# Twelve row tiles in place of nine, in room taken from the descriptor area of GpSimd's transfers

## The chip, the cores and the metric

The kernel runs on one core of a Trainium2 chip. A core has TensorE (PE in the profile, with its weight loads as PEld), VectorE (DVE), ScalarE (ACT), GpSimd (POOL) and SyncE (SP), which here does nothing but issue transfers between the chip's main memory (HBM) and the on-chip memory (SBUF). Matmuls write to a small memory of eight banks, PSUM. The metric is the device time of one execution in microseconds (us); the times shown are medians of several executions, and the profile is of one of them.

## The reference

One layer of an encoder over 2048 tokens of width 1024 (float32), with 256 memory tokens for the cross-attention. Every sub-layer is wrapped in two RMS norms:

```python
u = rms_norm(h, g_mix_pre);  z = u @ w_in                        # 1024 x 2816
y = concatenate([swa_with_sinks(qa, ka, va, sinks),              # windowed attention
                 hgrn2(qh, fh, ih, gh, lb, onorm)]) @ w_out      # gated recurrence
h = h + rms_norm(y, g_mix_post)
u = rms_norm(h, g_x_pre);    m = rms_norm(mem, g_mem)
h = h + rms_norm(cross_attention(u, m, wq, wk, wv, wo), g_x_post)
u = rms_norm(h, g_ffn_pre)
h = h + rms_norm((silu(u @ w_gate) * (u @ w_up)) @ w_down, g_ffn_post)   # 1024 x 2816 x 1024
```

## The kernel before

All large products are float32 with nearly full precision. Each operand is split into a high and a low part (`split2`, L982: ScalarE or GpSimd rounds the high part, VectorE subtracts it from the whole for the low part), and three matmuls per pair of 128-wide pieces give high x high, high x low and low x high (`products`, L1122 to L1124). Large products are also cut in two by two blocks and done with seven block products in place of eight, with sums and differences of blocks (`seven`, L1126; `streamed` and `combined` make the sums).

The layer is done in three stages. `in_first` (L451) and the stage behind it make the input projection, the windowed attention and the recurrence, and "the fold" (`fold_cross`, L272) multiplies the cross-attention's weights with the memory tokens into two 1024 x 1024 matrices, `qk` and `vo`, in HBM. Beyond the fold, from L253 on, the third stage runs `phases` (L1210) over a list of jobs (`jobs`, L1418): the output projection (`mixed_block`), the scores against `qk` (`score_block`), the values against `vo` (`value_block`), the two halves of the FFN's gate and up products (`hidden_blocks`) and three parts of its down product (`down_block`). Each job holds one operand in SBUF, the other streams by:

- **T tiles** are the resident operand, split. There are seven (four tagged "big", three tagged "T"). To make one, two halves are loaded into row tiles, split by ScalarE (`T<-row`, L985) and VectorE (`T<-row,T`, L988), and given up.
- **sraw** and **S tiles** are the streaming operand, raw and split. A block's `sraw` pair is loaded a block ahead, four such tiles exist, and the S tiles are split two steps ahead.
- **Row tiles** are buffers of 128 x 1024 float32, 4 KB in each partition. `row_tile` (L1458) hands them out in turn from one pool. They are the landing place of T halves and of rows of `x`, `h1` and `h2`, and the place where results are gathered, normed (`squared` L1494, `mean_square` L1472, L1529, L1604, L1617), transposed by TensorE (L1381) with a copy back by ScalarE (L1382), and stored. In the FFN's down part they also are summed into HBM by GpSimd's transfers (`add` L1503, `add_to` L1507), the only transfers that GpSimd issues. A load into a row tile must wait until the tile's last user, often a store, is done.
- **extra** is a single tile of the same size (L84), in which `combined` (L1025) makes the sums of the resident operands beside the earlier jobs and stores them (`qk_s`, `vo_s`, `u_s`, `d_s`; L1032).

`phases` takes each step's transfers, splits and follow-up work in an order written out in code, but the order on each engine is made by a scheduler, which takes the program, the dependencies and its own estimates of time, and places each instruction. SyncE issues its loads (`load`, L74) and stores (`store`, L77) strictly in the order that the scheduler gives, and an issue that must wait holds all that stand behind it.

SBUF is filled to the brim in the third stage. At its lowest addresses lies an area for the descriptors that GpSimd's transfers write, 16 KB of each partition unless the program says otherwise. `cm` (L403 to L408) is a small tile for a causal mask, made by VectorE and GpSimd between the first and the second stage.

Of the kernel before, what the change touches and what calls it, by code (L numbers as in the profile page):

```python
# [11 lines left out]
F32 = mybir.dt.float32  # L12
# [6 lines left out]
P = 128  # L19
T = 2048  # L20
D = 1024
# [27 lines left out]
class Layer:  # L49
# [1407 lines left out]

    def row_tile(self):  # L1458
        self._n += 1
        return self.st_pool.tile([P, D], F32, tag="row", name=f"row_{self._n}", bufs=9)  # L1460

    def rows_of(self, src, n):
        t = self.row_tile()
# [301 lines left out]
```

## Time and profile before

| | |
|---|---|
| median of three executions | 2584.7 us (2578.32 to 2585.96) |
| the profiled execution | 2583.14 us, of which the span from first to last instruction 2581.4 us |
| mean granted TensorE clock | 0.997 of full speed |
| TensorE busy | 2540.2 us, 98% of the span |
| VectorE, ScalarE, GpSimd busy | 1765.3, 1262.4 and 422.6 us |
| moved by transfers | 486.36 MB, 188 GB/s on average |

How to read it: in a row of grouped instructions, `out<-in` names what is written and read, by the program's names without buffer numbers; behind the count come the busy time and the mean of one in ns, then the idle time of the engine just before, and what ended it. In lists of waits, the columns are who waited, for whom, the total in us, how often, and the longest. In lists by time, the columns are start, duration, engine, line, operation; in brackets stands the idle time before and what ended it. In tables by stretch, busy time and count of each engine are followed by the granted clock, the share of the transfer engines' time and the rate.

### The profile page before, as it was taken

The page shows a single profiled execution, that of the slowest core. Times are in us where ns is not written, and L with a number is a line of the kernel's source. Part 1 is how long each engine was busy: PE and PEld are TensorE (multiplying, and loading weights), DVE is VectorE, ACT ScalarE, POOL GpSimd, SP SyncE. Part 2 cuts the span into 40 slices and gives each one's busy share as a digit, 9 for nine tenths or more (in the row PEclk, how much of TensorE's full clock was granted, in tenths as well). Part 3 has the DMA queues.
Part 4 walks back from the last instruction along what each step waited for, and adds up shares of the span by engine and source line. Part 5 has one row for each costly group of instructions (what it writes and reads, how often), then busy time and mean ns, then how long its engine had stood idle before and what let it go on. Part 6 is the DMA issues. An engine that isn't in the chain of part 4 may idle for free.

```text
span 2581.4 us, 34890 instructions
## 1 busy us (share of the span) xinstructions
PE 2540.2 (98%) x12326; PEld 2127.1 (82%) x12326; DVE 1765.3 (68%) x2791; ACT 1262.4 (49%) x2643; POOL 422.6 (16%) x612
## 2 busy tenths in 40 slices
PE   9999999999999999999999999999999999999998
PEld 8888888888988778888778888888888888888886
DVE  7785588987556778778885655566666557574766
ACT  5563466565555565565563333354333335453543
POOL 5231334321302232212300000000000000000022
PEclk9999999999999999999999999999999999999999
DMA  6445755765887886666973622253565425464886
GB/s 188 147 163 178 198 164 158 239 186 175 251 279 283 295 274 217 211 228 200 325 246 127 208 87 74 89 189 130 172 203 196 156 93 190 158 199 106 224 178 152
DMA packets 357295, 486.36 MB, mean 188 GB/s; under 512 B 20352, under 2 KB 248704, under 8 KB 357120
## 3 DMA queue, kind: packets, MB, share of 16 engines
q1 hardware_dynamic: 351072, 462.11, 54.7%
q0 software_dynamic: 6048, 22.02, 4.9%
q8 instruction: 97, 1.59, 0.3%
q14 instruction: 78, 0.64, 0.1%
HBM read 317.34 MB, written 166.72 MB: 188 GB/s over the span
## 4 chain that ended last, share of the span: by engine, by line
PE 83%; DMA 6%; DVE 5%; ACT 3%; issue 2%; SPq 0%; POOL 0%; DVEq 0%; POOLq 0%; ACTq 0%
PE psm L1122 23%; PE psm L1124 23%; PE psm L1123 23%; PE psg L158 2%; PE psg L157 2%; PE psg L156 2%; PE pss L1381 1%; ACT T L985 1%; DMA h1t_d<-row 1%; DMA raw<-in_wo_x_dram 1%; DVE S L988 1%; DMA x<-in_w_out_dram 1%; DMA z<-in_w_out_dram 1%; DMA kk<-z_d 0%; ACT junk L1476 0%
## 5 line engine op out<-in xcount | busy, mean ns | idle before, releaser
L1122 PE MATMUL psm<-T,S 128*128 128x512 f32 x2680 | 1038.3, 392 | 11.4 <-ACT part L1137 9.9
L1123 PE MATMUL psm<-T,S 128*128 128x512 f32 x2680 | 1043.9, 390 | 0.9 <-DVE T L988 0.8
L1124 PE MATMUL psm<-T,S 128*128 128x512 f32 x2680 | 1031.0, 390 | 4.4 <-DVE S L988 4.4
L1122 PEld LDWEIGHTS psm<-T,S 128*128 128x128 f32 x2680 | 504.0, 188 | 120.5 <-ACT part L1137 10.2
L1124 PEld LDWEIGHTS psm<-T,S 128*128 128x128 f32 x2680 | 503.7, 188 | 111.0 <-DVE S L988 6.1
L1123 PEld LDWEIGHTS psm<-T,S 128*128 128x128 f32 x2680 | 504.3, 188 | 105.4 <-DVE T L988 2.3
L985 ACT ACTIVATE S<-sum 128x512 fp32r<-128x512 f32 (+1 forms) x330 | 198.4, 618 | 364.4 <-PE psm L1124 269.5
L988 DVE TENSOR_TENSOR S<-sraw,S 128x512 fp32r<-128x512 f32 (+1 forms) x315 | 214.1, 687 | 227.9 <-ACT S L985 214.2
L988 DVE TENSOR_TENSOR S<-sum,S 128x512 fp32r<-128x512 f32 (+1 forms) x388 | 260.5, 680 | 44.9 <-ACT S L985 29.4
L1137 ACT ACTIVATE part<-psm 128x512 f32<-128x512 f32 x285 | 168.7, 596 | 242.4 <-PE psm L1124 222.6
L985 ACT ACTIVATE S<-sraw 128x512 fp32r<-128x512 f32 (+1 forms) x268 | 165.3, 618 | 105.1 <-PE psm L1124 95.1
L1509 POOL DMA_DIRECT2D y_d<-row x16 | 14.0, 876 | 1076.5 <-DVE row L1695 1025.3
L988 DVE TENSOR_TENSOR T<-row,T 128x1024 fp32r<-128x1024 f32 (+1 forms) x112 | 132.5, 1195 | 40.7 <-ACT T L985 40.4
L157 PE MATMUL psg<-u,whi 128*128 128x512 f32 x320 | 127.8, 399 | 0.0
L158 PE MATMUL psg<-u,wlo 128*128 128x512 f32 x320 | 127.1, 397 | 0.0
L156 PE MATMUL psg<-u,whi 128*128 128x512 f32 x320 | 127.1, 397 | 0.0
L1476 ACT ACTIVATE junk<-row 128x512 f32<-128x512 f32 x160 | 99.7, 624 | 52.3 <-DVE row L1498 31.8
L985 ACT ACTIVATE T<-row 128x1024 fp32r<-128x1024 f32 (+1 forms) x112 | 114.0, 1032 | 17.4 <-DMA row<-d_s 6.6
L987 POOL TENSOR_SCALAR S<-sum 128x512 fp32r<-128x512 f32 x58 | 51.7, 891 | 299.1 <-PE psm L1124 247.1
L1646 DVE TENSOR_TENSOR row<-psm,part 128x512 f32<-128x512 f32 x66 | 43.7, 688 | 68.4 <-PE psm L1124 68.4
L1655 DVE TENSOR_TENSOR part<-psm,part 128x512 f32<-128x512 f32 x66 | 43.8, 688 | 62.7 <-PE psm L1124 62.5
L1695 DVE TENSOR_TENSOR row<-psm,part 128x512 f32<-128x512 f32 x72 | 49.1, 688 | 51.1 <-PE psm L1124 51.0
(364 smaller groups left out, 3710.4 us busy)
## 6 DMA issues: line engine op xcount, KB each, us to landing
sraw<-in_w_gate_dram SPq DMA_DIRECT2D x44, 512.0 KB, 3.6
sraw<-in_w_up_dram SPq DMA_DIRECT2D x44, 512.0 KB, 3.6
hid_d<-row SPq DMA_DIRECT2D x44, 512.0 KB, 2.7
sraw<-hid_d SPq DMA_DIRECT2D x32, 512.0 KB, 4.1
sraw<-in_w_in_dram SPq DMA_DIRECT2D x44, 256.0 KB, 3.4
z_d<-pair SPq DMA_DIRECT2D x20, 512.0 KB, 2.9
raw<-in_w_in_dram SPq DMA_DIRECT2D x20, 512.0 KB, 4.9
z_d<-z SPq DMA_DIRECT2D x20, 512.0 KB, 3.7
```

Source lines behind the costliest of these rows:

```text
L156: nc.tensor.matmul(ps, ah, bh, start=(i == 0), stop=False)
L157: nc.tensor.matmul(ps, ah, bl, start=False, stop=False)
L158: nc.tensor.matmul(ps, al, bh, start=False, stop=(i == n - 1))
L985: self.nc.scalar.activation(hi, raw, AF.Copy)
L987: self.nc.gpsimd.tensor_scalar(hi, raw, 1.0, 1.0, ALU.mult, ALU.mult)
L988: self.nc.vector.tensor_tensor(lo, raw, f32(hi), ALU.subtract)
L1122: nc.tensor.matmul(ps, s[:, 0, k, :], t[:, 0, k, :], start=st, stop=False, **kw)
L1123: nc.tensor.matmul(ps, s[:, 0, k, :], t[:, 1, k, :], start=False, stop=False, **kw)
L1124: nc.tensor.matmul(ps, s[:, 1, k, :], t[:, 0, k, :], start=False, stop=sp, **kw)
L1137: nc.scalar.activation(t, ps, AF.Copy)
L1476: self.nc.scalar.activation(junk, a, AF.Square, scale=float(D) ** -0.5, accum_out=to)
L1695: nc.vector.tensor_tensor(d, a, b, ALU.add)
```

## The change

The pool of row tiles gets twelve buffers in place of nine, 12 KB more in each partition. The room comes from the descriptor area, which is set to 4096 bytes in place of the 16384 that it has without the argument. No other line is changed, but the scheduler makes the order anew from these sizes.

```diff
 def row_tile(self):
     self._n += 1
-    return self.st_pool.tile([P, D], F32, tag="row", name=f"row_{self._n}", bufs=9)
+    return self.st_pool.tile([P, D], F32, tag="row", name=f"row_{self._n}", bufs=12)
...
-    nc = _bacc.Bacc("TRN2", target_bir_lowering=False, num_devices=1)
+    nc = _bacc.Bacc("TRN2", target_bir_lowering=False, num_devices=1, dynamic_dma_scratch_size=4096)
```

In the new order the first 3,800 of TensorE's 11,250 rows (like instructions in a row are one) are the same. VectorE and GpSimd make `cm` a little earlier. In the third stage loads of row tiles move ahead of stores and of stream loads by one to five places on SyncE, above all around the starts of the score, the value and the first FFN job, and splits, transposes and copies follow them.

## The prediction

> **What bounds the kernel now.** I read the page first: its span and its first section.
>
> ```profile
> span 2581.4 us, 34890 instructions
> PE 2540.2 (98%) x12326; PEld 2127.1 (82%) x12326; DVE 1765.3 (68%) x2791; ACT 1262.4 (49%) x2643; POOL 422.6 (16%) x612
> ```
>
> TensorE is busy for 98% of the span, and nothing in the change adds or removes a matmul. All that the change can do is to fill, or to add to, the 41.2 us without one (2581.4 - 2540.2). So I asked next for the busy time by stretch, cut where the losses lie. The load queue's instructions in order of time show the first load of a row tile, at 782.6 us, and so the first cut.
>
> ```profile
> 782.58 0.80 SPq L75 DMA_DIRECT2D row<-out_s  x2
> ```
>
> ```profile
> core 0: us, PE busy (x) PEld busy (x) DVE busy (x) ACT busy (x) POOL busy (x), PEclk, DMA share, GB/s
> 0.00:782.00 782.00, 764.16 (x4348) 660.64 (x4349) 559.85 (x1065) 434.47 (x1035) 228.51 (x340) 1.00 0.63 195
> 782.00:890.00 108.00, 107.91 (x506) 89.34 (x505) 76.40 (x93) 59.08 (x131) 27.48 (x43) 1.00 0.82 285
> 890.00:900.00 10.00, 7.58 (x35) 6.01 (x34) 9.77 (x11) 3.98 (x9) 3.86 (x5) 1.00 0.93 325
> 900.00:950.00 50.00, 50.00 (x238) 41.63 (x237) 34.14 (x39) 29.94 (x68) 13.00 (x21) 1.00 0.86 272
> 950.00:980.00 30.00, 25.59 (x111) 20.13 (x110) 22.17 (x26) 17.54 (x32) 8.05 (x12) 0.89 0.84 305
> 980.00:1130.00 150.00, 149.86 (x720) 124.69 (x719) 115.36 (x209) 86.52 (x210) 40.01 (x55) 1.00 0.64 210
> 1130.00:1260.00 130.00, 128.98 (x608) 106.39 (x607) 109.19 (x143) 75.96 (x172) 35.38 (x48) 1.00 0.70 231
> 1260.00:1340.00 80.00, 75.32 (x346) 61.26 (x345) 69.99 (x79) 55.00 (x106) 17.90 (x25) 0.98 0.88 296
> 1340.00:1735.00 395.00, 395.00 (x1752) 327.23 (x1751) 231.15 (x347) 150.27 (x259) 0.00 (x0) 1.00 0.39 129
> 1735.00:1750.00 15.00, 14.21 (x62) 11.12 (x61) 14.24 (x19) 8.98 (x13) 0.00 (x0) 1.00 0.60 191
> 1750.00:2270.00 520.00, 520.00 (x2295) 430.52 (x2294) 328.89 (x500) 205.91 (x364) 0.00 (x0) 1.00 0.49 166
> ```
>
> From 782 to 2270 us TensorE lacks 0.09 + 2.42 + 0 + 4.41 + 0.14 + 1.02 + 4.68 + 0 + 0.79 + 0 = 13.6 us. In two stretches the granted clock is low as well: 11% of 30 us is 3.3 us, 2% of 80 us is 1.6 us. Together 18.5 us, 0.7% of the span: the ceiling of what more row tiles could bring before 2270 us. Stretches 950-980 (4.41 + 3.3 = 7.7 us) and 1260-1340 (4.68 + 1.6 = 6.3 us) hold most of it. Up to 782 us there are no row tiles at all.
>
> **What it removes: waits for a row tile.** In 950-980 I read the waits of ScalarE (from 900 on), those of the load queue, and then the instructions in order of time.
>
> ```profile
> ACT T L985 <- DMA row<-qk_s: 4.0, 2, 3.3
> ACT T L985 <- DMA row<-qk_d: 3.2, 2, 1.9
> ```
> ```profile
> SPq L75 <- DMA h1t_d<-row: 6.5, 1, 6.5
> SPq L75 <- DVE T L988: 4.7, 4, 2.0
> ```
> ```profile
> 955.47 0.33 SPq L78 DMA_DIRECT2D h1t_d<-row  x1
> 962.40 0.32 SPq L75 DMA_DIRECT2D row<-qk_s  x1
> 962.82 0.39 SPq L75 DMA_DIRECT2D sraw<-h1t_d  x1
> ...
> 966.89 1.06 ACT L985 ACTIVATE T<-row 128x1024 fp32r<-128x1024 f32 x1 [3.29 <-DMA row<-qk_s]
> ...
> 968.58 0.77 PE L1122 MATMUL psm<-T,S 128*128 128x512 f32 x1 [2.68 <-ACT part L1137]
> ```
>
> This is one chain. At 955.5 SyncE issues the store of a row tile. The next load wants that very tile, so the queue stands 6.5 us until the store has landed, and issues the load at 962.4. Its data land at 966.9, where ScalarE, which takes its work in order, has waited 3.3 us to split them. The copy out of PSUM (L1137) stands behind that split, and TensorE waits 2.68 us for the bank. With twelve tiles that load reuses a tile given up three allocations earlier. The changed kernel's order on SyncE says the same: five loads of qk_s and qk_d that stood behind this store or close to it now stand ahead of it, and the stream loads (sraw) behind them.
>
> Can the transfers carry them earlier? By tens of microseconds:
>
> ```profile
> 930.00:940.00 10.00, 10.00 (x50) 8.29 (x49) 5.08 (x6) 8.48 (x19) 3.08 (x7) 1.00 0.75 259
> 940.00:950.00 10.00, 10.00 (x46) 8.29 (x45) 9.26 (x10) 6.03 (x15) 2.69 (x1) 1.00 0.80 254
> 950.00:960.00 10.00, 8.44 (x46) 6.94 (x44) 6.70 (x9) 8.65 (x19) 5.46 (x9) 1.00 1.00 368
> 960.00:970.00 10.00, 7.18 (x27) 5.55 (x28) 9.75 (x9) 5.62 (x9) 2.28 (x1) 0.89 0.66 203
> ```
>
> The engines are full only from 950 to 960. Unused are 2.5 + 2.0 + 0 + 3.4 = 7.9 us, more than the 7.2 us (4.0 + 3.2) that ScalarE waited for these loads. So I take this stretch as won whole: **-7.7 us** (bounds 0, if no load lands sooner, and -7.7).
>
> The low clock belongs to it: gaps of 2.42 us at 893 us left it at 1.00, while here it fell to 0.89 for the stretch. The Trainium skill, "TensorE: Matmul & The Clock Gate", Part 1, says that the clock halves after an idle window of about 3.4 us. By that rule no single gap here is long enough, and the stretch would be worth 4.4 us; the trace shows the clock falling after a gap of 2.68 us, and the measurement decides.
>
> In 1260-1340 only a part is row tiles. The load queue's waits from 1296 to 1316, and the instructions in order:
>
> ```profile
> SPq L75 <- DVE T L988: 8.1, 4, 3.2
> ```
> ```profile
> 1260.07 0.69 DVE L1409 TENSOR_TENSOR row<-row 128x512 f32<-128x512 f32 x1 [2.15 <-DMA u_d<-row]
> ...
> 1311.86 0.50 PE L1122 MATMUL psm<-T,S 128*128 128x512 f32 x1 [2.05 <-ACT part L1137]
> ...
> 1332.28 0.50 PE L1123 MATMUL psm<-T,S 128*128 128x512 f32 x1 [0.76 <-DVE T L988]
> ```
>
> The first wait is for a store of the same tile that is then overwritten (L1409): no number of tiles helps. The second follows loads that waited 8.1 us for VectorE to finish with a tile; their splits then come in a bunch. It and the third cost 2.05 + 0.76 + 1.6 (clock) = 4.4 us. But ScalarE and VectorE are near full here, 55 and 70 of 80 us, so earlier loads spread the bunch only in part. Bounds 0 and -4.4; I take a third, **-1.5 us**, nearer to nothing since the engines are the tighter limit. At 893 us VectorE waits for the one `extra` tile:
>
> ```profile
> 889.67 1.66 DVE L1032 TENSOR_TENSOR extra<-extra,row 128x1024 f32<-128x1024 f32 x1 [2.56 <-DMA qk_s<-extra]
> ```
>
> That tile is not changed: 0. The rest (0.09 + 0.14 + 1.02 + 0.79 = 2.0 us) is small: 0.
>
> **What it adds and moves.** The scheduler was run again, so besides the loads, splits, transposes and sums of score and value blocks change places. On SyncE a stream load now stands behind row loads and stores that wait. The trace of before has no row for the stalls of a new order. Below, a stall is excluded by nothing, and its upper price is the dearest such chain here, 7.7 us; I take **+1.0 us**, the size of the small gaps that lie about (1.02 in 1130-1260).
>
> The mask tile `cm` is made earlier on VectorE and GpSimd, ahead of two weight splits. It ended this wait:
>
> ```profile
> 270.21 0.11 DVE L406 MEMSET cm<- 64x64 f32 x1 [9.37 <-POOL cm L405]
> ```
>
> VectorE had nothing to do then that TensorE lacked; the memset itself is 0.11 us. I take 0; ends: 1 us either way. All left-hand tiles move 12 KB down; no row shows a price of an address: 0.
>
> The smaller descriptor area concerns GpSimd's 42 transfers alone:
>
> ```profile
> q0 software_dynamic: 6048, 22.02, 4.9%
> y_d<-row POOLq DMA_DIRECT2D x16, 512.0 KB, 5.1
> out_dram<-row POOLq DMA_DIRECT2D x14, 512.0 KB, 6.5
> row<-y_d POOLq DMA_DIRECT2D x12, 512.0 KB, 8.2
> ```
> ```profile
> L1509 POOL DMA_DIRECT2D y_d<-row x16: 853/862/1107, 2289.6 to 2424.3; - x16
> ```
>
> They are 6048 / 42 = 144 packets each, 9 for each of 16 engines. The first is issued at 2289.6 us; the room of the 16 sums into y_d, which a smaller area would use again, is free by the landing time of 5.1 us after 2424.3, and the 26 others follow one by one. I take 0; above, one landing time, 8.2 us, if a late transfer had to wait for another and that one ended the kernel. The Trainium skill, "DMA: Bandwidth & Descriptors", Terms, gives a descriptor 16 bytes; by an estimate from that page 4096 bytes would be 256 descriptors, 28 transfers of 9. No run here shows what reuse costs.
>
> **The sum.** -7.7 - 1.5 + 1.0 = -8.2 us on the profiled execution's 2583.1 us (2581.4 of span and 1.7 around it): **2575 us**. That execution lies 1.6 us below the median of the three runs, 2584.7.
>
> **The rivals.**
> - Transfers, not tiles, set the end of 950-980. For it: 368 GB/s and a share of 1.00 at 950-960, right ahead of the gap; loads pulled forward then only queue in the engines. Against it: 0.66 to 0.80 around. Then nothing is won there, and -1.5 + 1.0 gives 2582.6, call it 2583. The Trainium skill, "DMA: Bandwidth & Descriptors", Specifications, puts a core's share of HBM at about 358 GB/s; the 368 here agrees that this window is at the limit.
> - Nearly all of it: the new order also takes the other losses of 1260-1340 (4.4) and the small ones (2.0), with no new stall: 2583.1 - 7.7 - 4.4 - 2.0 = 2569.
> - Slower: a stream load stands behind a row load that waits for its tile. It would happen where score blocks begin. In before the stream load was issued at 962.82 and its pair was first used at 979.80:
>
> ```profile
> 979.80 0.68 DVE L1097 TENSOR_TENSOR sum<-sraw,sraw 128x512 f32<-128x512 f32 x1
> ```
>   With a landing of 5 to 8 us that is some 9 us of slack; the new order puts two more stores and four loads ahead, one of which need only wait the 6.5 us above. From 9 us of delay on, TensorE stops. With the old gap closed, a new one like it, and another at the value blocks, cost 2 x 7.7 against the 7.7 won: 2583.1 + 7.7 = 2591.
>
> **How the numbers follow.** Forecast around 2575 (2571 to 2580): 0.45. Nearly all: 0.15. Transfers set the end: 0.20. Slower: 0.20. A measurement of this kernel can tell about 0.3% from no change, 7.8 us, so faster means below 2577 and slower above 2592.5. Faster: two thirds of the forecast and all of the second, 0.45. Slower: two thirds of the last, 0.14. The rest, 0.41, is within. The range takes in the middle cases and most of both ends: 2565 to 2590.
>
> **What would show it.** In the changed profile: TensorE busy for 29.5 us or more of the 30 around 950-980 and a clock of 1.00 there (the main step); SyncE's wait for h1t_d<-row gone from that stretch; ScalarE's waits for row<-qk_s and row<-qk_d below 2 us together; the wait at L1409 and that at L1032 still there; GpSimd's transfers at 0.9 us of issue and 5 to 8 us to landing as before. Wrong would be the step if the loads are issued earlier and land no earlier (transfers), and the sum if TensorE waits for a stream load.

## The result, and the profile after

| | before | after |
|---|---|---|
| median of 14 executions each | 2580.97 us | 2573.69 us |
| lowest to highest | 2577.73 to 2586.45 | 2568.62 to 2580.88 |
| the profiled execution | 2583.14 us | 2572.97 us |

The ratio of after to before is 0.9963, with a 95% interval of 0.9953 to 0.9973: the change saves 0.37% (0.27 to 0.47), about 9.5 us of the median of before. The medians are 7.3 us apart, the two profiled executions 10.2 us.

The page of after, its span and first section:

```profile
span 2571.3 us, 34876 instructions
...
PE 2535.4 (99%) x12326; PEld 2124.0 (83%) x12326; DVE 1764.8 (69%) x2791; ACT 1263.9 (49%) x2643; POOL 425.4 (17%) x612
```

TensorE now lacks 2571.3 - 2535.4 = 35.9 us, where it lacked 41.2. The busy time by stretch, cut at the same places as before, with the program's first 782 us ahead of the others:

```profile
0.00:782.00 782.00, 764.00 (x4349) 661.00 (x4350) 557.68 (x1065) 435.32 (x1035) 231.45 (x340) 1.00 0.63 195
```
```profile
782.00:890.00 108.00, 105.61 (x492) 87.12 (x491) 76.60 (x92) 59.02 (x130) 29.09 (x42) 1.00 0.81 285
890.00:900.00 10.00, 9.61 (x47) 7.74 (x46) 8.77 (x11) 4.39 (x9) 4.22 (x6) 1.00 0.92 338
...
950.00:980.00 30.00, 30.00 (x149) 24.86 (x149) 27.69 (x34) 24.19 (x53) 11.07 (x17) 1.00 0.83 291
...
1130.00:1260.00 130.00, 127.61 (x597) 105.11 (x598) 110.94 (x138) 73.55 (x166) 38.20 (x52) 1.00 0.70 226
1260.00:1340.00 80.00, 78.48 (x369) 63.87 (x368) 69.01 (x81) 56.33 (x108) 12.50 (x18) 1.00 0.82 278
...
sum 1488.00, PE 1479.69 PEld 1222.47 DVE 1022.95 ACT 703.47 POOL 145.49; mean PE 147.97 PEld 122.25 DVE 102.30 ACT 70.35 POOL 14.55
```

The last row sums the ten stretches from 782 to 2270 us: TensorE lacks 1488.00 - 1479.69 = 8.3 us there, and the granted clock is 1.00 in every one. Before it was 13.6 us idle and 4.9 us of low clock, 18.5. The difference, 10.2 us, is that of the two profiled executions. By stretch, idle and clock together:

| stretch, us | before | after | change |
|---|---|---|---|
| 782-890 | 0.1 | 2.4 | +2.3 |
| 890-900 | 2.4 | 0.4 | -2.0 |
| 950-980 | 7.7 | 0.0 | -7.7 |
| 1130-1340 | 1.0 + 6.3 | 2.4 + 1.5 | -3.4 |
| the other five | 0.9 | 1.6 | +0.7 |

In 950-980 the loads come earlier. The load queue's instructions of after in order of time; before, the load of `qk_s` that ended the wait was issued at 962.40:

```profile
947.21 2.43 SPq L75 DMA_DIRECT2D row<-qk_s  x2
950.75 1.09 SPq L75 DMA_DIRECT2D row<-qk_d  x2
...
954.85 0.33 SPq L78 DMA_DIRECT2D h1t_d<-row  x1
957.66 0.33 SPq L75 DMA_DIRECT2D row<-qk_s  x1
```

The sixth load of `qk_s`, which was issued behind that store at 962.40 and landed at 966.87 before, is now the second of the pair at 947.21: by the trace it is issued at 948.38 and has landed at 957.71. Two loads of `qk_d` (950.75) have passed the store as well, and the next load behind it is issued 2.8 us after it, not 6.9. What is left in 950-980 of the queue's wait for that store (total, how often, longest):

```profile
SPq L75 <- DMA h1t_d<-row: 2.1, 1, 2.1
```

ScalarE's waits for `row<-qk_s` (4.0 us) and `row<-qk_d` (3.2 us) are not in the list of after any more. The room on the transfer engines was used just where it was free:

```profile
930.00:940.00 10.00, 10.00 (x49) 8.28 (x49) 3.97 (x4) 7.89 (x18) 3.08 (x7) 1.00 1.03 387
```

From 930 to 940 us the share rose from 0.75 to 1.03 and the rate from 259 to 387 GB/s. New is a stall at 829.8 us. After's instructions there, the bracket naming the idle time before each:

```profile
821.13 0.36 SPq L75 DMA_DIRECT2D extra<-qk_d  x1
...
826.87 1.23 DVE L1032 TENSOR_TENSOR extra<-extra,row 128x1024 f32<-128x1024 f32 x1 [1.72 <-issue]
...
829.77 0.50 PE L1124 MATMUL psm<-T,S 128*128 128x512 f32 x1 [2.30 <-DVE S L988]
```

In the new order VectorE's sum of `qk` (L1032) stands ahead of the sums and splits of the stream, and its operand, loaded into the one `extra` tile, is issued at 821.1. That is as soon as the store that still held the tile (`qk_s<-extra`, issued at 817.49) has landed, at 821.07 by the trace; the operand lands at 826.79. VectorE waits 1.72 us with all that stands behind it, and TensorE waits 2.30 us for a split. Before, this sum waited too (2.22 us, at 829.01), but behind those splits, and TensorE lost nothing. The two waits that were to stay are there, in another place of the same order:

```profile
889.44 1.23 DVE L1032 TENSOR_TENSOR extra<-extra,row 128x1024 f32<-128x1024 f32 x1 [2.91 <-DMA qk_s<-extra]
...
893.66 0.50 PE L1124 MATMUL psm<-T,S 128*128 128x512 f32 x1 [0.39 <-DVE S L988]
...
1252.21 0.69 DVE L1409 TENSOR_TENSOR row<-row 128x512 f32<-128x512 f32 x1 [1.26 <-DMA u_d<-row]
...
1256.50 0.50 PE L1124 MATMUL psm<-T,S 128*128 128x512 f32 x1 [1.50 <-DVE S L988]
```

### The profile page after: what moved, and what is told of

Read it like the earlier page. It is cut to its first block, busy times and chain, and to the rows that moved or that the text cites. A ratio compares the mean times of both kernels' runs of the same rounds, so it can differ in the third digit from the quotient of the medians.

```text
span 2571.3 us, 34876 instructions
## 1 busy us (share of the span) xinstructions
PE 2535.4 (99%) x12326; PEld 2124.0 (83%) x12326; DVE 1764.8 (69%) x2791; ACT 1263.9 (49%) x2643; POOL 425.4 (17%) x612
## 4 chain that ended last, share of the span: by engine, by line
PE 82%; DMA 6%; DVE 6%; ACT 2%; issue 2%; POOL 1%; SPq 1%; DVEq 0%; POOLq 0%; ACTq 0%
PE psm L1122 22%; PE psm L1124 22%; PE psm L1123 22%; PE psg L157 2%; PE psg L156 2%; PE psg L158 2%; PE pss L1381 1%; DMA x<-in_w_out_dram 1%; DVE S L988 1%; DMA y_d<-sg 1%; DMA u_d<-row 1%; DVE T L988 0%; SPq L75 0%; DMA qk_s<-extra 0%; DVE S L808 0%
## 5 line engine op out<-in xcount | busy, mean ns | idle before, releaser
L1137 ACT ACTIVATE part<-psm 128x512 f32<-128x512 f32 x285 | 168.9, 596 | 244.9 <-PE psm L1124 223.6
L988 DVE TENSOR_TENSOR T<-row,T 128x1024 fp32r<-128x1024 f32 (+1 forms) x112 | 131.8, 1189 | 35.9 <-ACT T L985 34.1
```

What stands on the lines that cost most here:

```text
L988: self.nc.vector.tensor_tensor(lo, raw, f32(hi), ALU.subtract)
L1137: nc.scalar.activation(t, ps, AF.Copy)
```

## The experiments

My theory: loads of T halves wait for a row tile, and each further tile lets them run further ahead; the time comes out of 950 to 1340 us. Rivals: the smaller area itself moves the time; it is not the number of tiles but that loads share tiles with stores; the new order does it by chance, and another one would do as well. Every kernel below was timed against before in five rounds, each pair on one chip; the median of before differs between groups of runs (2581.55 to 2583.49 us), so it is the ratios that can be compared.

### The area alone, and ten and eleven tiles

area_only has nine row tiles as before, and this line alone is changed:

```diff
-    nc = _bacc.Bacc("TRN2", target_bir_lowering=False, num_devices=1)
+    nc = _bacc.Bacc("TRN2", target_bir_lowering=False, num_devices=1, dynamic_dma_scratch_size=4096)
```

rows10 sets `bufs=10` in `row_tile` and the area to 12288, rows11 `bufs=11` and 8192.

> Nine row tiles as before, the descriptor area at 4096 bytes; TensorE's order is that of before, only the mask tile is made earlier. Tiles theory (the time comes from loads that no longer wait for a row tile): no change, ratio 0.999 to 1.001, and the stretch 950-980 us still lacks about 4.4 us of TensorE with a low clock. Area theory (the smaller area, the moved addresses or the earlier mask tile give the time): ratio near 0.996.

> Ten row tiles, area 12288 bytes. Tiles theory: a third of the way or less, ratio 0.998 to 1.000, since one tile more moves the late load of 962.4 us by only one place; the gap near 960 us shrinks but stays. Order theory (each new order by the scheduler gains or loses by chance, the number of tiles does not matter): anything from 0.995 to 1.004, not in step with the number of tiles.

> Eleven row tiles, area 8192 bytes. Tiles theory: between ten and twelve, ratio 0.9965 to 0.999, TensorE's gap near 960 us below 2 us and its clock at 1.00. Order theory: anything from 0.995 to 1.004, not in step with the number of tiles.

| kernel | tiles, area | median, us | ratio to before |
|---|---|---|---|
| area_only | 9, 4096 | 2584.97 (before 2583.19) | 0.9998 (0.9988 to 1.0007) |
| rows10 | 10, 12288 | 2579.2 | 0.9986 (0.9976 to 0.9996) |
| rows11 | 11, 8192 | 2577.68 | 0.9975 (0.9965 to 0.9985) |
| after | 12, 4096 | 2573.69 | 0.9963 (0.9953 to 0.9973) |

From nine to twelve tiles each brings about 0.12%, 3 us, though the intervals of neighbours overlap. The stretch 950-980 of area_only, rows10 and rows11:

```profile
950.00:980.00 30.00, 25.05 (x114) 19.99 (x113) 23.61 (x27) 18.75 (x36) 6.67 (x11) 0.94 0.89 314
```
```profile
950.00:980.00 30.00, 26.17 (x120) 21.46 (x119) 24.08 (x27) 19.81 (x41) 8.34 (x14) 0.94 0.86 310
```
```profile
950.00:980.00 30.00, 27.83 (x133) 22.73 (x132) 25.75 (x32) 22.70 (x48) 13.12 (x17) 1.00 0.74 264
```

TensorE's busy time rises from 25.05 to 26.17, 27.83 and, in after, 30.00 us. ScalarE's waits from 945 to 985 us of area_only and of rows10:

```profile
ACT T L985 <- DMA row<-qk_d: 3.4, 2, 1.8
...
ACT T L985 <- DMA row<-qk_s: 3.2, 1, 3.2
```
```profile
ACT T L985 <- DMA row<-qk_d: 4.2, 2, 2.9
```

With nine tiles both waits of before are there, with ten one of them, with eleven (whose list has none) neither. TensorE's only wait of that stretch in rows11 is for a split by GpSimd, which has nothing to do with row tiles (the last section):

```profile
PE psm L1122 <- POOL S L987: 2.2, 1, 2.2
```

So in this stretch the waits for loads are gone with eleven tiles already, and rows11 missed the gap of under 2 us that was expected of it by another cause. What the twelfth tile adds is not shown: the intervals of rows11 and after overlap.

The area alone does nothing that can be measured, with TensorE's and ScalarE's orders those of before. So the time comes with the tiles and not with the area. Each number of tiles has an order of its own from the scheduler, and no run had twelve tiles in the order of before; what speaks against chance is the series, which goes in step with the number, and the waits that leave with it.

### A smaller area, and a thirteenth tile

rows12_small is after with an area of 1024 bytes, and has its order on every engine; rows13 has thirteen row tiles, for which the area must shrink to 640:

```diff
-        return self.st_pool.tile([P, D], F32, tag="row", name=f"row_{self._n}", bufs=9)
+        return self.st_pool.tile([P, D], F32, tag="row", name=f"row_{self._n}", bufs=13)
...
-    nc = _bacc.Bacc("TRN2", target_bir_lowering=False, num_devices=1)
+    nc = _bacc.Bacc("TRN2", target_bir_lowering=False, num_devices=1, dynamic_dma_scratch_size=640)
```

> Twelve row tiles as in the changed kernel, in the same order, but an area of 1024 bytes, so that its room must be used again many times by the 42 transfers. Tiles theory with a free area: the same as the changed kernel, ratio 0.9953 to 0.9973, GpSimd's transfers at 0.9 us of issue and 5 to 8 us to landing. Area has a price: GpSimd's issue of a transfer grows beyond 1 us or landings beyond 8 us, and if the last ones end the kernel, up to 8 us more (ratio up to 0.9995).

> Thirteen row tiles, area 640 bytes. Tiles theory: the waits for a row tile that cost TensorE time are gone with twelve already, so nothing more: ratio 0.9955 to 0.9975. If more tiles go on helping: the rest of 1260-1340 us (1.5 us) and small gaps go, ratio 0.994 to 0.9955. Order theory: anything from 0.993 to 1.002.

rows12_small: 2573.14 us, 0.9958 (0.9945 to 0.9971), no different from after. rows13: 2581.7 us, 1.0003 (0.9993 to 1.0012): all is lost again. Its 950-980 is still near full (29.84 us busy), and the loss is at the other end of the program:

```profile
2400.00:2555.00 155.00, 150.05 (x655) 123.39 (x654) 102.09 (x138) 72.87 (x144) 30.70 (x44) 0.99 0.77 185
```

In before and after TensorE is busy for all 155 us of that last stretch; here it lacks 5 us. That is where GpSimd's transfers are, so the area of 640 bytes came under suspicion, and was tried by itself below.

### Four tiles for the loads alone

In loads4 the T halves land in four tiles of their own (at all three places that load them), and all else in eight; the area is 4096.

```diff
-        return self.st_pool.tile([P, D], F32, tag="row", name=f"row_{self._n}", bufs=9)
+        return self.st_pool.tile([P, D], F32, tag="row", name=f"row_{self._n}", bufs=8)
+    def half_tile(self):
+        self._n += 1
+        return self.st_pool.tile([P, D], F32, tag="half", name=f"half_{self._n}", bufs=4)
...
-                            half(g, self.row_tile)
+                            half(g, self.half_tile)
```

> The same twelve tiles in two groups: four only for the halves of T tiles, eight for all else. Theory (it is loads queued behind stores of results in one round of tiles that cost the time): the T loads never wait for a store now, the gap near 960 us stays closed, and the ratio is like that of the changed kernel, 0.995 to 0.998. Rival (what counts is how many loads can be ahead): four tiles hold the loads back to four ahead, the waits of ScalarE for row loads come back, and the ratio is 0.999 to 1.006.

2590.84 us, 1.0035 (1.0020 to 1.0049): slower than before with the same twelve tiles. Parting loads from stores did close most of the gap at 950-980 (28.44 us busy, clock 1.00, no wait for `h1t_d<-row`), but time was lost elsewhere, so the idea that it is enough missed. TensorE lacks 2.7 us in 782-890 (at a clock of 0.98) and 4.6 in 2400-2555 (0.99), where before lacks 0.1 and 0 at 1.00. ScalarE's waits of loads4 from 2400 to 2450 us, where before waits 2.4 us for its halves of `d_s`, never over 0.8 at once:

```profile
ACT T L985 <- DMA half<-d_s: 5.9, 4, 3.1
ACT T L985 <- DMA half<-in_w_down_dram: 5.8, 3, 2.2
```

Right behind the longest of them TensorE waits 3.47 us (at 2432.40) for a copy (L1137) that stands behind ScalarE's splits. Four tiles hold two pairs of halves, and no more can be ahead. In one pool of twelve a burst of loads may take more than four when stores are few, and stores when loads are few. So how many loads can be ahead counts as well; but all else had eight tiles here, one fewer than the nine of before, and no run tells the two losses apart.

### A second extra tile

rows9_extra2 has nine row tiles and rows11_extra2 eleven, both with an area of 4096; rows12_extra2 has twelve and an area of 640. All three have

```diff
-        return self.st_pool.tile([P, D], F32, tag="extra", name=f"extra_{self._n}", bufs=1)
+        return self.st_pool.tile([P, D], F32, tag="extra", name=f"extra_{self._n}", bufs=2)
```

> Nine row tiles as before, two extra tiles, area 4096 bytes. Theory: the wait at 893 us (2.4 us) goes, the gap at 950-980 us (7.7 us) stays, since that is the row tiles': ratio 0.998 to 1.000. Rival (any 4 KB more for any tile gives the gain, by the new order): ratio 0.997 or less.

> The changed kernel with two extra tiles in place of one (area 640 bytes to make room); nearly the same order on TensorE. Theory: what is left near 829 us (2.3 us of TensorE) and 893 us (0.4 us) is VectorE standing for the one extra tile, whose store or load it waits for; with two these waits go, and the kernel is 2 to 3 us faster than the changed one: ratio to before 0.9945 to 0.996. Rival: VectorE waits for the transfers' speed, not for the tile; then the same waits come at the same places and the ratio is that of the changed kernel, 0.996 to 0.997.

> Eleven row tiles and two extra tiles, with a descriptor area of 4096 bytes. Theory (the single extra tile holds VectorE's order at about 830 and 890 us in the kernels with many row tiles, and the second tile takes that wait away; the area is large enough): about 1 to 3 us under the kernel with eleven row tiles alone (0.9975), so 0.9963 to 0.9972, with no TensorE wait over 1 us between 820 and 900 us. Rival (what a second extra tile gives at 830 us the scheduler's order takes elsewhere): 0.9975 or above.

rows9_extra2: 2580.03 us, 0.9993 (0.9983 to 1.0003): no gain by itself that can be measured. TensorE's wait at 893 us shrinks from 2.42 to 0.94 us (now at 889.6), and in 950-980 TensorE still lacks 3.5 us, at a clock of 1.00 (7.7 us were expected to stay, clock included). rows12_extra2: 2581.95 us, 1.0002 (0.9989 to 1.0015). rows11_extra2: 2577.63 us, 0.9965 (0.9950 to 0.9980), a hair under rows11's 0.9975 and within both intervals. The stretches of rows12_extra2:

```profile
782.00:890.00 108.00, 107.90 (x503) 89.26 (x501) 76.70 (x94) 57.06 (x124) 28.91 (x37) 1.00 0.82 295
...
2400.00:2555.00 155.00, 150.22 (x650) 123.21 (x649) 99.70 (x135) 74.98 (x144) 30.00 (x44) 0.98 0.77 184
```

and 950-980 of rows11_extra2, which has 107.91 us busy in 782-890:

```profile
950.00:980.00 30.00, 27.80 (x132) 22.93 (x132) 24.72 (x30) 22.12 (x50) 14.97 (x17) 0.94 0.83 296
```

So the second tile does take the stall at 830 us away: 107.9 us busy, where after has 105.61. Every kernel here with ten tiles or more in one pool and one `extra` tile has a wait of 1.2 to 2.9 us there, those with two have none. In rows12_extra2 the loss of 4.8 us in the last stretch, with a clock of 0.98, eats that and more. Again the area is 640 bytes.

### The area of 640 bytes by itself, and the two losers with 1024

rows12_a640 is after with `dynamic_dma_scratch_size=640`. rows12_extra2_a1024 and rows13_a1024 are rows12_extra2 and rows13 with 1024; their room comes from the 16-wide small tiles and from two tiles that nothing reads:

```diff
-        return self.sm.tile([P, w], F32, tag=role, name=f"{role}_{self._n}")
+        return self.sm.tile([P, w], F32, tag=role, name=f"{role}_{self._n}", bufs=2 if w == 16 else 3)
...
-            for pool in (self.cst, edge):
-                nc.gpsimd.memset(pool.tile([P, 24], F32, name="pad"), 0.0)
```

> Twelve row tiles as in the changed kernel, with the descriptor area at 640 bytes in place of 4096; the order on TensorE is that of the changed kernel. Theory (an area of 640 bytes holds two of GpSimd's transfers, and a third waits for the first): in the last stretch, about 2500 to 2530 us, the third transfer of a group waits some 3.7 us before it is issued, the accumulating load row<-y_d behind it lands late, TensorE loses about 5 us near 2530, and the time is some 7 us over the changed kernel's: a ratio to before of 0.998 to 1.000. Rival (the area is free at any size, and the thirteen-row and the two-extra kernels lost by their order): no such wait, and the changed kernel's ratio, 0.9953 to 0.9973.

> Twelve row tiles and two extra tiles with a descriptor area of 1024 bytes; the room comes from two tiles of 96 bytes that hold nothing and from the 16-wide small tiles, which have two buffers in place of three. Theory (the kernel with twelve row and two extra tiles lost its gain to the 640-byte area alone): the 3.7 us wait of the third transfer near 2510 us is gone, the 2.3 us wait at 830 us is gone too, and the time is 1 to 4 us under the changed kernel's: a ratio to before of 0.9945 to 0.9960. Rival (the order made for two extra tiles loses elsewhere): 0.997 or above.

> Thirteen row tiles with a descriptor area of 1024 bytes, room from the same small tiles. Theory (the kernel with thirteen row tiles lost to the 640-byte area): near the changed kernel, 0.9955 to 0.9975, with no wait of a third transfer near 2510 us. Rival (a thirteenth tile costs by the order it brings): 0.999 or above.

| kernel | rows, extra, area | median, us | ratio to before |
|---|---|---|---|
| rows12_a640 | 12, 1, 640 | 2586.26 | 1.0001 (0.9990 to 1.0013) |
| rows12_extra2_a1024 | 12, 2, 1024 | 2575.12 | 0.9952 (0.9936 to 0.9968) |
| rows13_a1024 | 13, 1, 1024 | 2575.9 | 0.9968 (0.9953 to 0.9983) |

Before had 2583.49 us in this group. rows12_a640 has the instructions of after in the same order on every engine; only the area differs, and the whole gain is gone. GpSimd's transfers of one group, in after and then in rows12_a640:

```profile
2503.88 0.96 POOL L1509 DMA_DIRECT2D out_dram<-row  x1 [1.62 <-DVE row L1739]
2504.63 1.15 POOL L1505 DMA_DIRECT2D row<-y_d  x1
2505.67 1.01 POOL L1509 DMA_DIRECT2D out_dram<-row  x1
```
```profile
2509.25 0.97 POOL L1509 DMA_DIRECT2D out_dram<-row  x1 [1.73 <-DVE row L1739]
2509.89 1.27 POOL L1505 DMA_DIRECT2D row<-y_d  x1
2514.91 0.88 POOL L1509 DMA_DIRECT2D out_dram<-row  x1 [3.75 <-DVE sum L1097]
2517.62 0.88 POOL L1505 DMA_DIRECT2D row<-y_d  x1 [1.84 <-issue]
```

The third is issued 1.8 us after the first in after, and 5.7 us after it in rows12_a640. The bracket names a sum of VectorE that the transfer doesn't read. The row of these stores in rows12_a640 (count, size, median us from issue to landing) shows what lasts so long, the landing of the first:

```profile
out_dram<-row POOLq DMA_DIRECT2D x14, 512.0 KB, 5.4
```

So an area of 640 bytes has room for two of these transfers, and a third waits until the first has landed. The landing times in the trace bear it out: in all four such groups the third is issued 0.31 us after the first has landed, and never are more than two in flight, where after has three and before up to four. Behind it the fourth, which adds `y_d` onto a row tile, comes late as well. Who pays, in rows12_a640:

```profile
2527.41 0.63 ACT L1476 ACTIVATE junk<-row 128x512 f32<-128x512 f32 x1 [7.35 <-DMA row<-y_d]
...
2535.33 0.76 PE L1122 MATMUL psm<-T,S 128*128 128x512 f32 x1 [4.51 <-DVE part L1139]
```

ScalarE's squares wait 7.35 us for that sum, the norm (L1739) waits with them, the sums of VectorE stand behind the norm, and TensorE loses 4.51 us and then some of its clock:

```profile
2400.00:2555.00 155.00, 150.49 (x654) 123.80 (x653) 101.59 (x137) 74.21 (x144) 30.70 (x44) 0.98 0.78 186
```

4.5 us idle and 2% of 155, 3.1 us, make 7.6. With 1024 bytes both losers recover, in the same order of all instructions (the two that write the unread tiles apart). The last stretch of rows12_extra2_a1024:

```profile
2400.00:2555.00 155.00, 155.00 (x685) 128.08 (x684) 106.37 (x144) 76.55 (x150) 32.25 (x48) 1.00 0.79 190
```

rows12_extra2_a1024 has the lowest ratio of all, 0.9952, and in its profile the stall at 830 us is gone as well; but its interval and that of after (0.9953 to 0.9973) overlap, so it is not shown to be faster than after. A thirteenth tile adds nothing to the twelfth that can be measured.

## Why the prediction was right

The forecast was 2575 us, the median came out at 2573.69; the direction, the place and the mechanism of the main step held. Some terms were off in size and partly cancel; that the total came so close is in part luck. Of its steps:

- **The bound and the ceiling: right.** All of the difference between the two profiled executions (10.2 us) came out of the 18.5 us of 782 to 2270. The first 782 us have 764.00 us of TensorE, before 764.16.
- **-7.7 for 950-980: right, and to the tenth in the profiled execution** (30.00 us busy, clock 1.00). The series shows the cause: from nine to eleven tiles ScalarE's waits for the halves leave one after the other. One sign was forecast too strongly: the queue's wait for `h1t_d<-row` did not go, it fell from 6.5 to 2.1 us. And -7.7 is not what every execution gets: rows12_small, with the order of after, has 27.20 us there, by a cause that has nothing to do with row tiles (the last section).
- **The low clock belongs to the gaps: right, but not by their length alone.** It is 1.00 in all ten stretches of after from 782 to 2270 us, and 0.94 where rows10 and area_only keep gaps of up to 2.41 and 2.56 us:

```profile
969.29 0.79 PE L1122 MATMUL psm<-T,S 128*128 128x512 f32 x1 [2.41 <-ACT T L985]
```
```profile
961.64 0.53 PE L1122 MATMUL psm<-T,S 128*128 128x512 f32 x1 [2.56 <-ACT part L1137]
```

  In rows11_extra2 a single gap of 2.19 us goes with 0.94, while in rows12_small one of 2.79 us (last section) leaves 1.00:

```profile
968.96 0.50 PE L1122 MATMUL psm<-T,S 128*128 128x512 f32 x1 [2.19 <-POOL S L987]
```
```profile
950.00:980.00 30.00, 27.20 (x132) 22.43 (x131) 25.06 (x30) 20.98 (x44) 12.73 (x15) 1.00 0.65 234
```

  What else decides is open.
- **-1.5 for 1260-1340, a third of 4.4: too small.** The wait at L1409 shifted from 1260.07 to 1252.21, into the stretch before, so the two are read together: 7.3 us before, 3.9 after, -3.4. SyncE's wait of 8.1 us for VectorE's splits into T tiles has left the list of 1296 to 1316 us, and with it the gap of 2.05 us and the low clock. The near full ScalarE and VectorE, which the prediction took for the tighter limit, were not: VectorE is busy for 69.01 of 80 us now and 69.99 before, with the gap closed.
- **The extra tile at 893 us, 0: wrong in size.** VectorE waits as before (2.91 us in place of 2.56), but TensorE loses 0.39 in place of 2.42: 2.0 us won that were not forecast. The step equated VectorE's wait with TensorE's; the new order moved work between the two, and the wait found cover. Which of the moved instructions gives the cover was not tried.
- **+1.0 for stalls of a new order: too small.** One stall alone, at 829.8 us, costs 2.3, the quiet stretches 0.7 more. It is one extra tile's, as the kernels with ten tiles or more and two of them show (107.9 us busy in place of 105.61).
- **0 for the smaller area: right** at 4096 bytes (area_only 0.9998) and at 1024. But the working behind it was not: the estimate of nine descriptors of 16 bytes, from the Trainium skill ("DMA: Bandwidth & Descriptors", Terms), would have let 640 bytes hold four such transfers (640 / 16 / 9 = 4.4). The runs show two. And the last 26 transfers do not follow one by one, as the prediction took it: in before up to four are in flight at once. The upper bound of 8.2 us, one landing, has its like in rows12_a640: 7.6 us of TensorE's time in the profile, 0.38% or some 10 us by the ratios (1.0001 and 0.9963).

Together: -7.7 - 3.4 - 2.0 + 2.3 + 0.7 = -10.1 us on the profiled execution, where -8.2 was forecast; errors of -1.9, -2.0 and +2.0, two of which cancel. The medians moved by 7.3.

The rivals: **transfers set the end** is out, since the loads landed earlier (the sixth of `qk_s` by 9.2 us) and the engines took 387 GB/s at 930 to 940 us, where they had room; so the 368 GB/s that this rival took for the limit was not one. **Slower, by a stream load behind a waiting row load**, did not happen: the longest wait for `h1t_d<-row` in 950-980 was 2.1 us, under the 9 us of slack. **Nearly all** (2569) went too far: the profiled execution, 2572.97, is nearer to 2575, since 3.9 of the 7.3 us of 1130-1340 stayed and a new stall came, which this rival ruled out.

## What to carry to other kernels

When an engine that takes its work in order waits for a load, look at what holds the load's issue: here a queue that could not hand out a buffer, and from nine to twelve buffers each was worth some 3 us on average, while a thirteenth was worth nothing that could be measured. Buffers in one shared pool did more than the same number parted by use. Room that no instruction seems to use can be taken, but only down to what is in flight at once: count how many are in flight at the busiest place, and try one size below the one that you want, so that the edge is known.

## What the runs showed of the hardware that was not expected

**The area of GpSimd's transfers has a hard edge.** 4096 and 1024 bytes are the same in time (0.9963 and 0.9958), 640 costs all that twelve tiles brought (1.0001). Yet an area of 1024 bytes holds transfers back as well, one later. In rows12_small the first of a group lands at 2509.07 and the fourth is issued 0.31 us behind that, although ScalarE's part of the row that it reads (L1699) was done at 2508.70:

```profile
2509.38 0.91 POOL L1505 DMA_DIRECT2D row<-y_d  x1 [2.66 <-ACT S L985]
```

None of the kernels with 1024 bytes has more than three in flight, and TensorE lost nothing by it. If each transfer takes the same room, two but not three in 640 bytes and three but not four in 1024 make it, by an estimate from these runs, more than 256 and at most 320 bytes, about twice the 144 bytes of 9 descriptors in the prediction's estimate.

**VectorE can shut GpSimd out for several instructions.** In rows12_small TensorE's only wait in 950-980 is for one of GpSimd's splits, which took 5.80 us; of the 58 of its kind the median is 0.626 us. GpSimd's split, VectorE's last two instructions beside it and TensorE's wait:

```profile
959.66 5.80 POOL L987 TENSOR_SCALAR S<-sum 128x512 fp32r<-128x512 f32 x1 [5.57 <-PE psm L1124]
...
964.29 0.68 DVE L988 TENSOR_TENSOR S<-sraw,S 128x512 fp32r<-128x512 f32 x1
964.89 0.68 DVE L1557 TENSOR_TENSOR row<-psm,part 128x512 f32<-128x512 f32 x1
...
965.51 0.50 PE L1122 MATMUL psm<-T,S 128*128 128x512 f32 x1 [2.79 <-POOL S L987]
```

VectorE ran without a gap, with instructions that read two operands from SBUF, from before 959.66 to 964.89. The split ended at 965.46, within the first instruction that reads one of its two from PSUM (L1557, 964.89 to 965.57). rows11 (5.17 us) and rows11_extra2 (5.20 us) have the same picture, with a loss of TensorE of 2.2 us in each. The split of rows11_extra2:

```profile
963.71 5.20 POOL L987 TENSOR_SCALAR S<-sum 128x512 fp32r<-128x512 f32 x1 [5.57 <-PE psm L1124]
```

In after the same split took 1.13 us, and there it was VectorE's instruction beside it that was longer:

```profile
964.35 1.13 POOL L987 TENSOR_SCALAR S<-sum 128x512 fp32r<-128x512 f32 x1 [5.03 <-PE psm L1124]
...
964.92 1.63 DVE L1530 TENSOR_TENSOR row<-row,row 128x1024 f32<-128x1024 f32 x1
```

Of its kind the others beside it take 1.21 us. The Trainium skill, "SBUF — State Buffer", SBUF: two separate sides, says that VectorE and GpSimd share a pair of ports under an exclusive lock, which a VectorE instruction with two SBUF inputs holds against a GpSimd one that reads SBUF. The rows agree, with up to 5.2 us of blocking; that GpSimd did not get in between several such instructions in a row goes beyond the sentence. Spans on GpSimd are rough and no experiment took the VectorE work away, so this is read from the traces and not shown by an edit. It would explain why kernels with the same order differ by 2.8 us in 950-980: it depends on which of the two is first by a fraction of a microsecond.
